# Tree-masked attention on one Trainium2 core: two halves of a PSUM bank for the transposed queries, and VectorE's V copies dealt evenly over the pairs

## The chip, the cores and the metric

The kernel runs on one core of a Trainium2 chip. The metric is the device time in microseconds (us) of one execution. A core has five engines that run their own instruction queues and wait for each other by semaphores: TensorE (PE in the profile; PEld is its weight load), VectorE (DVE), ScalarE (ACT), GpSimd (POOL) and SyncE (SP). Matmul results go to PSUM, everything else to SBUF; DMA engines move data between the chip's main memory and SBUF. Here nearly all DMAs are issued by POOL.

## The reference

Eight batches of twelve heads, 512 positions, 64 dimensions. Position i sees itself and its ancestors in a binary heap (parent of i is (i-1)//2), nothing else.

```python
scores = np.einsum('bhqd,bhkd->bhqk', Q, K) * scale      # scale = 1/8
scores = scores + (1 - mask) * (-1e9)                    # mask: self and ancestors
weights = np.exp(scores - np.max(scores, axis=-1, keepdims=True))
weights = weights / (np.sum(weights, axis=-1, keepdims=True) + 1e-10)
return np.einsum('bhqk,bhkd->bhqd', weights, V).astype(np.float32)
```

## The kernel before

The work is cut into 48 pairs of heads, six per batch. Since a query sees at most ten keys, the kernel doesn't compute all 512 x 512 scores. A first block of 128 keys (the upper levels of the tree) is scored against all 512 queries; the rest of the keys is met only by those queries that can have them as ancestors. Masks are added on TensorE by small code matrices (ctile) that put a large negative number where a query doesn't see a key.

Per pair i there are three functions:

- transposes(i): TensorE transposes Q (tile tq in PSUM, 8 matmuls, L293) and K (tile tk, 8 matmuls, L293). VectorE copies tq to the SBUF tile qt (L313), ScalarE copies tk to kt (L314). Both PSUM tiles have one buffer.
- scores(i): TensorE makes st (the first block, two matmuls with codes and two with qt and kt) and stx (the rest), all L339; ScalarE takes their exponentials to et (L352) and etx (L363). The PSUM tiles have one buffer each.
- values(i): TensorE multiplies et with v1 and etx with vx to o in PSUM (L391). A column of ones in v1 and vx gives the sums. VectorE takes the reciprocal (rec, L400) and the product (of, L405; called mult below).

V arrives in the staging tile vs as it lies in memory; its rows must be moved to other partitions. For a batch that is six copies by VectorE to vx ("big" in spread(), L279) and four by POOL to v1 ("small", also L279). Batches 0 and 1 do this in two halves of six heads (tile rows of 768 elements a partition), later batches all at once (1536). values() of a pair needs all six copies of its half or batch: batch 0's second half from pair 3 on, batch 1's halves from pairs 6 and 9, batch 2 from pair 12, batch 3 from pair 18.

The order of the instructions on TensorE, VectorE, ScalarE and POOL is that of the program text. The main loop over pairs is:

```python
            if i >= 4 and i + 2 < N:
                transposes(i + 2)
            if i + 1 < N:
                scores(i + 1)
            values(i)
            ...
            if i < 4:
                transposes(i + 2)
            for b, h0, h1, n0, n1 in deal.get(i, []):
                copies(spread(b, h0, h1)[0][n0:n1])
```

So from pair 4 on VectorE's order is qt(i+2), rec(i), mult(i), V copies of pair i. The dictionary deal says which of the six copies of which batch come in which pair: three in pairs 1 and 2 (batch 0's second half), 4 and 5, 7 and 8 (batch 1), 10 and 11 (batch 2); none in 0, 3, 6, 9 and 12; one in 13 to 16 and two in 17 (batch 3); then one in each pair to 41. The first six copies, batch 0's first half, come before the loop, after transposes(1).

POOL issues the loads (L233), up to twelve pairs ahead, and the stores (L412), which lag ten pairs behind while there are still loads; the last two pairs are stored by SP. The loads convert float32 to bf16 on the way.

Of the kernel before, what the change touches and what calls it, by code (L numbers as in the profile page):

```python
# [125 lines left out]
def kernel(  # L126
# [7 lines left out]
    nc = tc.nc  # L134
    B, H, S, D = Q.shape
    P = nc.NUM_PARTITIONS
    assert (S, D) == (512, 64) and H % 2 == 0
    T = 4
    HP = H // 2
# [4 lines left out]
    bf16 = mybir.dt.bfloat16  # L144
# [55 lines left out]
    psumT = ctx.enter_context(tc.tile_pool(name="psumT", bufs=1, space=PSUM))  # L200
    psumO = ctx.enter_context(tc.tile_pool(name="psumO", bufs=1, space=PSUM))


    plan = [(0, Q, 0, 0, 4), (0, K, 0, 0, 4), (0, V, 0, 0, 6),
            (0, Q, 0, 4, 8), (0, K, 0, 4, 8), (0, V, 0, 6, H),
# [3 lines left out]
    for b in range(2, B):  # L209
        at = HP * b - 2  # L210
        n = 4 if b < 3 else 6
# [5 lines left out]
        n = 8 if n == 4 else 6  # L217
        cuts = (n, H) if b < B - 1 else (n, 8, 10, H)
# [31 lines left out]
    def pick(v, t0, t1):  # L250

        stop = t1 + (1 if t1 > t0 else -1)
        return v[:, :, t0:stop if stop >= 0 else None:t1 - t0, :]

    def spread(b, h0, h1):
        vs = loaded["v", b]
        v1, vx = v1s[b % NV], vxs[b % NV]
        v = vs[:, h0:h1, :].rearrange("p h (t d) -> p h t d", t=T)
        big = [
            (vx[64:P, h0:h1, 0:3:2, 0:D], v[64:P, :, 0:3:2, :]),  # L260
            (vx[0:64, h0:h1, 1:4:2, 0:D], v[64:P, :, 1:4:2, :]),
        ]
        for part, c, t0, t1 in ((0, 0, 1, 2), (32, 0, 3, 0), (64, 1, 2, 1),
                                (96, 1, 0, 3)):
            assert KORD[XW[c] + part // 32] == (t0, 1)
            assert KORD[XW[c + 2] + part // 32] == (t1, 1)
            big.append((
                vx[part:part + 32, h0:h1, c:c + 3:2, 0:D],
                pick(v[32:64], t0, t1),
            ))  # L270
        small = [
            (v1[32 * r:32 * r + 32, h0:h1, 0:D], v[0:32, :, KORD[K1 + r][0], :])
            for r in range(T)
        ]
        return big, small

    def copies(ops, eng=None):
        for o, i in ops:
            (eng or nc.vector.tensor_copy)(out=o, in_=i)  # L279

    pairs = [(b, hp) for b in range(B) for hp in range(HP)]
    N = len(pairs)
    state, done, stored = {}, {}, []

    def transposes(i):
        b, hp = pairs[i]
        qs, ks = loaded["q", b], loaded["k", b]
        tq = psumT.tile([P, 512], bf16)
        tk = psumT.tile([P, 576], bf16)

        def put(o, src, t, mat):
            for hi in range(2):
                nc.tensor.matmul(  # L293
                    out=o[D * hi:D * hi + D], rhs=perms[mat],
                    lhsT=src[:, 2 * hp + hi, D * t:D * t + D],
                    start=True, stop=True, is_transpose=True,
                )

        for t in range(T):
            put(tq[:, P * t:P * t + P], qs, t, 0)  # L300
        for t in range(T):
            at = kput[t][1]
            if at[1] - at[0] == 32:
                step, run = at[2] - at[0], 64
            else:
                step, run = at[1] - at[0], 32
                assert at[2] - at[1] == step
            o = tk[:, at[0]:]
            o = bass.AP(o.tensor, o.offset, [list(o.ap[0]), [step, P // run], [1, run]])
            put(o, ks, t, 1 + t)  # L310
        qt = work.tile([P, 512], bf16)
        kt = work.tile([P, 512], bf16)
        nc.vector.tensor_copy(out=qt[:, :], in_=tq[:, :])  # L313
        nc.scalar.copy(  # L314
            out=kt[:, :].rearrange("d (i j x) -> d i j x", j=2, x=32),
            in_=tk[:, :].rearrange("d (j i x) -> d i j x", j=2, x=32)[:, 0:8],
        )
        state[i] = (qt, kt)

    def used(a):  # L320
        return a.rearrange("d (t p) -> d t p", t=T)[:, :, 32:P]

    def meeting(a, c):


        if c == 0:
            return a[:, 64:192]
        if c == 1:
            return a[:, 0:384].rearrange("d (n x) -> d n x", n=2)[:, :, 0:64]
        return a[:, P * c + 32:P * c + P]  # L330

    def scores(i):
        b, hp = pairs[i]
        q_, k_ = state[i]
        st1 = psumS.tile([P, 2, 512], fp32)
        stx = psumS.tile([P, 2, 512], fp32)

        def mm(dst, lhsT, rhs, first):
            nc.tensor.matmul(  # L339
                out=dst, lhsT=lhsT, rhs=rhs, start=first, stop=True,  # L340
                skip_group_check=not first,
            )

        hb = [slice(D * hi, D * hi + D) for hi in range(2)]
        q = [q_[hb[hi], :] for hi in range(2)]
        k = [k_[hb[hi], :] for hi in range(2)]
        for hi in range(2):
            mm(st1[:, hi, :], ck1[hb[hi], :], cq1[hb[hi], :], True)
        for hi in range(2):
            mm(st1[:, hi, :], k[hi][:, 32 * K1:32 * K1 + P], q[hi], False)  # L350
        et1 = et1pool.tile([P, 2, 512], bf16)
        nc.scalar.activation(  # L352
            out=et1[:, :, :], in_=st1[:, :, :], func=AF.Exp, scale=scale
        )
        for hi in range(2):
            mm(used(stx[:, hi, :]), ckx[hb[hi], :], cqx[hb[hi], :], True)
        for c in range(T):
            for hi in range(2):
                mm(meeting(stx[:, hi, :], c),
                   k[hi][:, 32 * XW[c]:32 * XW[c] + P],  # L360
                   meeting(q[hi], c), False)
        etx = etxs[i % NX]
        nc.scalar.activation(  # L363
            out=etx[:, :, :, 32:P],
            in_=stx[:, :, :].rearrange("p h (t q) -> p h t q", t=T)[:, :, :, 32:P],
            func=AF.Exp, scale=scale,
        )
        state[i] = (et1, etx)
# [40 lines left out]
    def store(eng, i, n):  # L409

        b, hp = pairs[i]
        eng.dma_start(  # L412
            out=out[b, 2 * hp:2 * hp + 2 * n].rearrange(
                "h (p t) d -> p h (t d)", t=T
            ),
            in_=done[i // 2][:, 2 * (i % 2):2 * (i % 2) + 2 * n, :],
        )
        stored.append(i)

    E = mybir.EngineType  # L420
    with tc.manual_schedule(engines={E.PE, E.DVE, E.Activation, E.Pool}):

        deal = {1: [(0, 6, H, 0, 3)], 2: [(0, 6, H, 3, 6)],
                4: [(1, 0, 6, 0, 3)], 5: [(1, 0, 6, 3, 6)],
                7: [(1, 6, H, 0, 3)], 8: [(1, 6, H, 3, 6)]}
        for b in range(2, B):
            cuts = ((4, 0, 3), (5, 3, 6)) if b == 2 else (
                (1, 0, 1), (2, 1, 2), (3, 2, 3), (4, 3, 4), (5, 4, 6))
            if b > 3:
                cuts = tuple((n, n, n + 1) for n in range(HP))  # L430
            for hp, n0, n1 in cuts:
                deal.setdefault(HP * (b - 1) + hp, []).append((b, 0, H, n0, n1))
        load(0, 14)
        transposes(0)
        scores(0)
        transposes(1)
        copies(spread(0, 0, 6)[0])
        for i in range(N):
            at_pair[0] = i
            load(i + AHEAD, FIRST[i] if i < len(FIRST) else None)  # L440
            upto = i - LATE if i + AHEAD < N - 1 else i - 1
            while 2 * len(stored) + 1 <= min(upto, N - 3):
                store(nc.gpsimd, 2 * len(stored), 2)
# [5 lines that stand above are left out]
            if i >= N - 2:  # L449
                store(nc.sync, i, 1)  # L450
            if i < 4:
                transposes(i + 2)
            for b, h0, h1, n0, n1 in deal.get(i, []):
                copies(spread(b, h0, h1)[0][n0:n1])
        assert not plan and not jobs

# [30 lines left out]
```

## Time and profile before

| | |
|---|---|
| median of 8 runs | 139.97 us (139.51 to 144.16) |
| the profiled execution's own time | 138.85 us |
| its span, first to last instruction | 137.1 us |
| TensorE busy | 109.3 us (80%) |
| ScalarE busy | 107.8 us (79%) |
| VectorE busy | 100.1 us (73%), of which V copies 38.1 (60 of them) |
| POOL busy | 90.3 us (66%) |
| DMA moved | 32.11 MB, mean 234 GB/s |
| rec(0), rec(12), rec(18), last rec | 15.28, 52.52, 66.86, 133.11 us |

Time inside the span is counted from its first instruction. rec(i) is the start of pair i's reciprocal, a convenient mark of progress: the first twelve pairs take 3.1 us each, the other 35 take 2.3. In a group's line of the profile stand the source line, the engine, the operation, output and inputs by tile name, the shape, the count, and then the busy time in us, the mean duration in ns and the engine's idle time before it.

### The profile page before, as it was taken

The page shows a single profiled execution, that of the slowest core. Times are in us where ns is not written, and L with a number is a line of the kernel's source. Part 1 is how long each engine was busy: PE and PEld are TensorE (multiplying, and loading weights), DVE is VectorE, ACT ScalarE, POOL GpSimd, SP SyncE. Part 2 cuts the span into 40 slices and gives each one's busy share as a digit, 9 for nine tenths or more (in the row PEclk, how much of TensorE's full clock was granted, in tenths as well). Part 3 has the DMA queues.
Part 4 walks back from the last instruction along what each step waited for, and adds up shares of the span by engine and source line. Part 5 has one row for each costly group of instructions (what it writes and reads, how often), then busy time and mean ns, then how long its engine had stood idle before and what let it go on. Part 6 is the DMA issues. An engine that isn't in the chain of part 4 may idle for free.

```text
span 137.1 us, 5468 instructions
## 1 busy us (share of the span) xinstructions
PE 109.3 (80%) x2400; PEld 79.6 (58%) x2400; DVE 100.1 (73%) x214; ACT 107.8 (79%) x145; POOL 90.3 (66%) x119
## 2 busy tenths in 40 slices
PE   0079687779957658998899998999889997999950
PEld 0035465556735536675677776776657675677630
DVE  4017668489797896979998897889877786975641
ACT  3027478697947965998899998999889997999940
POOL 6979895893697993339847397456944799921020
PEclk9999999999999999999999999999999999999995
DMA  4999999999999999999999999999999999999962
GB/s 79 162 188 196 196 197 196 198 197 198 197 199 196 204 193 198 198 253 225 197 318 241 274 202 206 338 228 259 197 265 294 248 294 274 386 391 387 360 243 99
DMA packets 41815, 32.11 MB, mean 234 GB/s; under 512 B 1280, under 2 KB 38784, under 8 KB 41792
## 3 DMA queue, kind: packets, MB, share of 16 engines
q0 software_dynamic: 41008, 30.94, 124.7%
q1 hardware_dynamic: 784, 0.84, 2.3%
q8 instruction: 18, 0.29, 0.8%
q14 instruction: 5, 0.04, 0.1%
HBM read 38.06 MB, written 12.58 MB: 369 GB/s over the span
## 4 chain that ended last, share of the span: by engine, by line
PE 49%; DVE 31%; ACT 6%; issue 6%; DMA 4%; POOL 1%; POOLq 0%
PE o L391 18%; DVE vx L279 16%; PE st L339 11%; DVE of L405 9%; PE stx L339 8%; PE tq L293 7%; PE tk L293 5%; DMA ks<-in_K_dram 4%; DVE qt L313 3%; ACT etx L363 3%; DVE rec L400 3%; ACT kt L314 2%; ACT et L352 1%; POOL qs L233 1%; POOLq L471 0%
## 5 line engine op out<-in xcount | busy, mean ns | idle before, releaser
L352 ACT ACTIVATE et<-st 128x1024 bf16<-128x1024 f32 x48 | 49.6, 1034 | 3.8 <-PE st L339 3.4
L314 ACT COPY kt<-tk 128x512 bf16<-128x512 bf16 x48 | 28.4, 592 | 19.3 <-PE tk L293 19.1
L279 DVE COPY vx<-vs 32x1536 bf16<-32x1536 bf16 (+3 forms) x60 | 38.1, 635 | 1.6
L363 ACT ACTIVATE etx<-stx 128x768 bf16<-128x768 f32 x48 | 39.2, 817 | 0.0
L405 DVE TENSOR_TENSOR of<-o,rec 128x512 f32<-128x512 f32 x48 | 33.2, 691 | 1.7
L279 POOL COPY v<-vs 32x768 bf16<-32x768 bf16 (+1 forms) x40 | 30.0, 750 | 2.7 <-DMA vs<-in_V_dram 0.9
L293 PE MATMUL tq<-ptile,qs 128*64 128x128 bf16 x384 | 19.9, 224 | 13.8 <-DVE qt L313 7.0
L391 PE MATMUL o<-vx,etx 128*64 128x65 bf16 (+1 forms) x576 | 26.8, 198 | 4.0 <-DVE vx L279 3.8
L412 POOL DMA_DIRECT2D out_dram<-of x23 | 18.2, 794 | 15.4 <-DVE of L405 8.2
L313 DVE COPY qt<-tq 128x512 bf16<-128x512 bf16 x48 | 20.0, 416 | 9.7 <-PE tq L293 9.0
L339 PEld LDWEIGHTS <-kt 64*128 64x128 bf16 x480 | 20.3, 96 | 10.6 <-ACT kt L314 3.5
L233 POOL DMA_DIRECT2D qs<-in_Q_dram x21 | 17.1, 813 | 13.3 <-PE o L391 4.0
L400 DVE RECIPROCAL rec<-o 128x8 f32<-128x8 f32 x48 | 9.8, 205 | 20.1 <-PE o L391 18.7
L293 PEld LDWEIGHTS <-qs 128*64 128x64 bf16 x384 | 15.2, 111 | 15.5 <-issue 8.0
L391 PEld LDWEIGHTS <-etx 128*64 128x64 bf16 (+1 forms) x576 | 19.5, 105 | 7.6 <-issue 5.0
L293 PE MATMUL tk<-ptile,ks 128*64 128x128 bf16 x384 | 20.3, 223 | 2.0 <-issue 1.3
L391 PE MATMUL o<-v,et 128*128 128x65 bf16 x384 | 20.4, 195 | 1.6 <-DVE of L405 1.1
L233 POOL DMA_DIRECT2D ks<-in_K_dram x21 | 16.6, 792 | 7.5 <-DMA vs<-in_V_dram 3.0
L339 PE MATMUL st<-qt,kt 64*128 64x512 bf16 x96 | 18.7, 386 | 2.0 <-DVE qt L313 1.8
L339 PE MATMUL st<-ctile 64*128 64x512 bf16 x96 | 19.2, 396 | 0.2 <-ACT et L352 0.2
L339 PEld LDWEIGHTS <-ctile 64*128 64x128 bf16 x192 | 11.3, 94 | 12.7 <-issue 1.8
L339 PE MATMUL stx<-qt,kt 64*128 64x96 bf16 (+1 forms) x384 | 17.8, 213 | 0.0
(13 smaller groups left out, 57.9 us busy)
## 6 DMA issues: line engine op xcount, KB each, us to landing
out_dram<-of POOLq DMA_DIRECT2D x23, 512.0 KB, 10.2
vs<-in_V_dram POOLq DMA_DIRECT2D x6, 768.0 KB, 15.8
qs<-in_Q_dram POOLq DMA_DIRECT2D x9, 384.0 KB, 15.7
ks<-in_K_dram POOLq DMA_DIRECT2D x9, 384.0 KB, 15.2
qs<-in_Q_dram POOLq DMA_DIRECT2D x9, 256.0 KB, 11.0
ks<-in_K_dram POOLq DMA_DIRECT2D x9, 256.0 KB, 11.5
vs<-in_V_dram POOLq DMA_DIRECT2D x4, 384.0 KB, 9.9
out_dram<-of SPq DMA_DIRECT2D x2, 256.0 KB, 2.1
```

The lines of the kernel that those rows point to most:

```text
L233: nc.gpsimd.dma_start(out=loaded[kind, b][:, h0:h1, :], in_=src[b, h0:h1].rearrange("h (p t) d -> p h (t d)", t=T),)
L279: (eng or nc.vector.tensor_copy)(out=o, in_=i)
L293: nc.tensor.matmul(out=o[D * hi:D * hi + D], rhs=perms[mat], lhsT=src[:, 2 * hp + hi, D * t:D * t + D], start=True, stop=True, is_transpos ...
L313: nc.vector.tensor_copy(out=qt[:, :], in_=tq[:, :])
L314: nc.scalar.copy(out=kt[:, :].rearrange("d (i j x) -> d i j x", j=2, x=32), in_=tk[:, :].rearrange("d (j i x) -> d i j x", j=2, x=32)[:, 0:8],
L339: nc.tensor.matmul(out=dst, lhsT=lhsT, rhs=rhs, start=first, stop=True, skip_group_check=not first,)
L352: nc.scalar.activation(out=et1[:, :, :], in_=st1[:, :, :], func=AF.Exp, scale=scale)
L363: nc.scalar.activation(out=etx[:, :, :, 32:P], in_=stx[:, :, :].rearrange("p h (t q) -> p h t q", t=T)[:, :, :, 32:P], func=AF.Exp, scale= ...
L391: nc.tensor.matmul(out=o2[p0:p1, hi, (D + 1) * t:(D + 1) * (t + 1)], lhsT=e[:, hi, P * t + p0:P * t + p1], rhs=v, start=hi not in (m[0] fo ...
L400: nc.vector.reciprocal(out=rec[:, :, :, :], in_=o4[:, :, :, D:D + 1])
L405: nc.vector.tensor_tensor(out=of4, in0=o4[:, :, :, 0:D], in1=rec[:, :, :, :].to_broadcast([P, 2, T, D]), op=ALU.mult,)
L412: eng.dma_start(out=out[b, 2 * hp:2 * hp + 2 * n].rearrange("h (p t) d -> p h (t d)", t=T), in_=done[i // 2][:, 2 * (i % 2):2 * (i % 2) + ...
```

## The change

Three edits, all in the order and the addresses of work; no instruction is added or removed.

1. The PSUM tile tq is no longer allocated per pair: one tile tqs of 2 x 512 bf16 elements is made once, and pair i uses its half i % 2. Both halves together are 2,048 bytes per partition.
2. The dictionary deal gives two V copies to each of pairs 0 to 11 and one to each of pairs 12 to 41.
3. Before the loop, four of the first six V copies come ahead of transposes(1), two after it.

```diff
+    tqs = psumT.tile([P, 2, 512], bf16)
...
     def transposes(i):
         b, hp = pairs[i]
         qs, ks = loaded["q", b], loaded["k", b]
-        tq = psumT.tile([P, 512], bf16)
+        tq = tqs[:, i % 2, :]
         tk = psumT.tile([P, 576], bf16)
...
-        nc.vector.tensor_copy(out=qt[:, :], in_=tq[:, :])
+        nc.vector.tensor_copy(out=qt[:, :], in_=tq)
...
-        deal = {1: [(0, 6, H, 0, 3)], 2: [(0, 6, H, 3, 6)],
-                4: [(1, 0, 6, 0, 3)], 5: [(1, 0, 6, 3, 6)],
-                7: [(1, 6, H, 0, 3)], 8: [(1, 6, H, 3, 6)]}
-        for b in range(2, B):
-            cuts = ((4, 0, 3), (5, 3, 6)) if b == 2 else (
-                (1, 0, 1), (2, 1, 2), (3, 2, 3), (4, 3, 4), (5, 4, 6))
-            if b > 3:
-                cuts = tuple((n, n, n + 1) for n in range(HP))
-            for hp, n0, n1 in cuts:
-                deal.setdefault(HP * (b - 1) + hp, []).append((b, 0, H, n0, n1))
+        deal = {}
+        for i in range(N):
+            b, hp = pairs[i]
+            if i < 9:
+                nb, h0, h1 = ((0, 6, H), (1, 0, 6), (1, 6, H))[i // 3]
+                deal[i] = (nb, h0, h1, 2 * (i % 3), 2 * (i % 3) + 2)
+            elif i < 12:
+                deal[i] = (2, 0, H, 2 * (i % 3), 2 * (i % 3) + 2)
+            elif b + 1 < B:
+                deal[i] = (b + 1, 0, H, hp, hp + 1)
         load(0, 14)
         transposes(0)
         scores(0)
+        big = spread(0, 0, 6)[0]
+        copies(big[:4])
         transposes(1)
-        copies(spread(0, 0, 6)[0])
+        copies(big[4:])
...
-            for b, h0, h1, n0, n1 in deal.get(i, []):
+            if i in deal:
+                b, h0, h1, n0, n1 = deal[i]
                 copies(spread(b, h0, h1)[0][n0:n1])
```

## The prediction

> **What bounds the kernel now.** I read the page first, then the chain of waits by stretch, then VectorE in order of time, then the DMA engines.
>
> The page's slices, DMA busy share in tenths and rate moved:
> ```profile
> DMA  4999999999999999999999999999999999999962
> GB/s 79 162 188 196 196 197 196 198 197 198 197 199 196 204 193 198 198 253 225 197 318 241 274 202 206 338 228 259 197 265 294 248 294 274 386 391 387 360 243 99
> ```
> The DMA engines never rest from about 5 to 130 us. While there are only loads (up to 57 us) they move a flat 197 GB/s; when only stores are left (116 to 127 us) some 386. Both are plateaus: the queue is full, and what is moved later can't be moved faster. So the kernel has two clocks, the compute pipeline and the DMA backlog, and a gain in the first counts only as far as the second lets it.
>
> The compute side in pairs 4 to 11, the chain of waits from 27.8 to 52.6 us, by line:
> ```profile
> by line: DVE vx L279 47.6%; DVE of L405 16.7%; PE o L391 12.2%; PE st L339 4.3%; DVE rec L400 4.2%; DVE qt L313 3.9%; PE tq L293 3.7%; issue 3.0%; PE stx L339 2.9%; PE tk L293 1.8%
> ```
> Nearly half of this stretch is V copies (L279) on VectorE. In order of time, pairs 7 to 9 of it (start, duration, instruction):
> ```profile
> 36.49 2.53 DVE L279 COPY vx<-vs 64x768 bf16<-64x768 bf16 x3
> 38.95 0.40 DVE L313 COPY qt<-tq 128x512 bf16<-128x512 bf16 x1
> 39.28 0.18 DVE L400 RECIPROCAL rec<-o 128x8 f32<-128x8 f32 x1
> 39.50 0.69 DVE L405 TENSOR_TENSOR of<-o,rec 128x512 f32<-128x512 f32 x1
> 40.22 1.85 DVE L279 COPY vx<-vs 32x768 bf16<-32x768 bf16 x3
> 42.10 0.42 DVE L313 COPY qt<-tq 128x512 bf16<-128x512 bf16 x1
> 42.66 0.21 DVE L400 RECIPROCAL rec<-o 128x8 f32<-128x8 f32 x1
> 42.91 0.69 DVE L405 TENSOR_TENSOR of<-o,rec 128x512 f32<-128x512 f32 x1
> 43.52 0.41 DVE L313 COPY qt<-tq 128x512 bf16<-128x512 bf16 x1
> 44.88 0.21 DVE L400 RECIPROCAL rec<-o 128x8 f32<-128x8 f32 x1 [0.94 <-PE o L391]
> ```
> From one reciprocal to the next: a pair with three V copies takes 3.4 us (39.28 to 42.66), its neighbour without any 2.2, and there VectorE idles 0.94. That is the unevenness that the new deal spreads. The same stretch's waits (us, times, longest):
> ```profile
> PE tq L293 <- DVE qt L313: 4.4, 3, 1.9
> DVE rec L400 <- PE o L391: 3.3, 3, 1.4
> PE o L391 <- DVE vx L279: 2.2, 2, 1.4
> ```
> The first is what the two halves are aimed at, the second is VectorE's idle time in the pairs without copies, the third is values() held by the last of three copies.
>
> Then the end, TensorE, load, VectorE, ScalarE, POOL, clock, DMA share and GB/s by stretch:
> ```profile
> 125.00:127.50 2.50, 2.50 (x66) 1.87 (x62) 1.60 (x5) 2.50 (x4) 0.76 (x1) 1.00 1.02 401
> 127.50:130.00 2.50, 2.25 (x40) 1.42 (x38) 1.66 (x4) 2.45 (x5) 0.00 (x0) 1.00 0.93 362
> 130.00:132.50 2.50, 1.38 (x37) 1.11 (x37) 0.94 (x3) 1.64 (x2) 0.75 (x1) 1.00 0.52 211
> 132.50:135.00 2.50, 0.57 (x19) 0.40 (x15) 0.90 (x2) 0.00 (x0) 0.00 (x0) 0.65 0.46 171
> 135.00:137.10 2.10, 0.00 (x0) 0.00 (x0) 0.00 (x0) 0.00 (x0) 0.00 (x0) 0.50 0.35 122
> ```
> Only here does the backlog run out and the DMA wait for compute. From 127.5 on 0.91 + 0.53 + 0.43 + 0.26 = 2.1 MB are moved; at the plateau of 386 GB/s that is 5.5 us, so the bytes alone would be done by 133.0, against about 135.8 now. **At most 2.8 us can be won at the end**, however early compute is.
>
> **The change part by part.** Times are of the profiled execution, which took 138.85 us with a span of 137.1; the median of the runs shown is 139.97, 1.1 above it. I carry the difference over to the median.
>
> *The halves (tqs).* The same 384 transposes and 48 copies of L313 (416 ns) remain; only the address alternates. Row first: TensorE waits 7.0 us in all for L313 before transposes, 8 times. If the wait went, pair i+3's transposes could start beside qt(i+2)'s copy; of the 7.0 us perhaps 0.5 is on the path, since behind the transposes the scores still need the same qt. The Trainium skill, "PSUM — Partial Sum Buffer", section "PSUM bank collisions raise a hardware error", speaks against it: TensorE writing and VectorE reading one bank in the same partitions collide also at different addresses, so PSUM must be guarded by bank, not by address. Both halves are one bank (2 x 1,024 bytes; the page gives 2 KiB per bank). No run here shows such an overlap. By the rule a safely guarded program keeps the wait and the halves bring 0; by the row 0.5. I take 0.
>
> *The prologue.* Now qt(1) ends at 11.65 and six copies follow, 11.69 to 14.69; values(0) waits for the last (TensorE goes on at 14.74). The first V half lands at 9.9 us (issued 2.89, 7.0 to landing), where VectorE is idle. After: four copies from 9.97, beside POOL's own V copies until 12.09. The nearest row is 64x768 beside POOL copies, 0.92 and 0.88 at 36.49, against 0.61 and 0.70 now; I take 0.8 twice, then 0.45 twice: until about 12.6. qt(1) queues behind them and ends at 13.0 in place of 11.65; scores(1), which began at 12.30 on ScalarE's kt, begins at 13.05; values(0), behind it on TensorE, begins at 14.3 in place of 13.54, and its second part, no longer held by copies, at 14.65 against 14.74. So 0. If every copy costs its undisturbed 0.36, qt(1) is hardly late: -0.55. If all are at 0.9: +0.6. A second rule speaks against this part. Row: matmul st takes 605 ns at 12.30 and 387 at 15.62; the durations step down near 13.8 (the clock column reads 1.00 on both sides, so the durations decide). "TensorE: Matmul & The Clock Gate", section "Part 1: The HAM clock gate", says that the clock doubles after a busy window of about 3.4 us. The new hole in TensorE's work, from about 12.2 to 13.05, lies in just that window, and one without a switch would cost another 3.4 us at the slow clock. In the slow stretch st to o takes 1.24 us (12.30 to 13.54), in the fast 0.68: by the rule up to 0.75 for about 1.3 pairs, by the trace 0 as long as the switch comes. I take 0 and keep 0.75 for the range.
>
> *Pairs 0 to 2.* Two copies each instead of 0, 3, 3. Pair 0 idled 1.57 us on VectorE before its next reciprocal: two copies (0.36 to 0.77) hide there. Pair 2 loses its third copy, which held values(3): the pair goes from 3.30 to the chain's 2.83 (mult, qt, st, stx, o, as in pairs 0 and 1): -0.45.
>
> *Pairs 3 to 11.* 18 copies, two a pair instead of 3, 3, 0. They took 2.64 + 4.31 + 4.82 = 11.8 us, 0.65 each. Pair 3's two hide in the 1.42 us idle before rec(4). From rec(4), 27.86, to rec(12), 52.52, is 24.66 us. After, VectorE has 8 x 1.36 (mult, qt, rec with gaps) and 16 copies at 0.65: 10.9 + 10.5 = 21.4. values(6), (9), (12) still wait for the last copy of their V, with VectorE idle about 0.2 each: 22.0. **-2.7.** No DMA or POOL instruction is moved.
>
> *Pairs 12 and 17.* Pair 12's new copy hides in 0.95 us idle; pair 17 loses one that took 0.55 or 1.08: -0.8. Later pairs are the same.
>
> Sum for compute: 0 - 0.45 - 2.7 - 0.8 = -3.95 by pair 18.
>
> *What then binds.* The loads keep their order behind a full queue, so they don't land earlier. The thinnest later lead is K of batch 6's second half: issued 88.51, landed 15.7 later at 104.2, used at 108.60: 4.4 us. 4.0 just fits. At the end the last mult would be done at about 130 instead of 134, with 1.1 MB still queued until 133.0: the 2.8 binds, less a few tenths because the last store is not spread evenly over the engines. Sum: **-2.45**, span 134.6, and 137.5 for the median.
>
> **The rivals.**
> A. *Compute gains less than the backlog would let through*: the prologue goes wrong with the slow clock (+1.35) and copies get dearer, a gain of 1 to 2: 138.0 to 139.0. For it: qt(1) does go behind four copies. Against: 3.95 leaves a reserve of 1.5.
> B. *Slower: each V copy collides with POOL.* A copy alone is 0.35 (768) or 0.55 (1536), beside POOL up to 0.92 and 1.08. POOL is busy 19.9 of 24.7 us in this stretch; copies in every pair could meet it each time. 16 copies at full price are 10 x 0.92 + 6 x 1.08 = 15.7, 5.2 over the sum: the 3.95 are gone and 1.2 is lost, 141.2. It decides from a mean of 0.9 per copy; now it is 0.65, and POOL's idle 32.2 to 35.5 us, where pairs 6 and 7 get copies, speaks against it.
> C. *No change*: the backlog ends later than I read it, or the early gain is lost to load leads: 140. Against: the DMA share falls to 0.5 after 130.
> D. *The halves do lift the wait*: 0.5 more for compute, swallowed by the same end: 137.3.
>
> **How the numbers follow.** A measurement of this kernel tells about 0.2% (0.28 us) from no change. Main case with D 0.62 (136.7 to 138.0), A 0.18, C 0.06, B 0.14. Faster 0.62 + 0.18 = 0.80, same 0.06, slower 0.14. The range starts at 136.6, the end's full 2.8 and some scatter of the median, and goes up through A to 139.5, leaving out C and B.
>
> **What would show it.** Right: about 2.2 to 2.9 us from each reciprocal to the next through pairs 4 to 11, none near 3.6; rec(12) at 48 to 50 us; waits of rec for o in 27.8 to 52.6 mostly gone; tq still waiting for qt; the DMA share near 1.0 until 132 or so, and the last store's wait for mult short against the backlog. qt(1) at 12 to 13 us. Wrong: V copies of 0.9 in every pair (B); transposes that wait for K before pair 40; a last mult at 130 with the DMA still idle afterwards, or a clock switch at 17 us.

## The result and the profile after

| | before | after |
|---|---|---|
| median | 139.51 us (53 runs, 137.78 to 144.80) | 137.73 us (18 runs, 137.30 to 138.08) |
| ratio after / before | | 0.9925, 95% interval 0.9905 to 0.9946 |
| profiled execution's own time | 138.85 us | 137.55 us |
| its span | 137.1 us | 135.8 us |
| rec(4), rec(12), rec(18), last rec | 27.86, 52.52, 66.86, 133.11 | 27.63, 48.49, 61.97, 130.16 |
| V copies on VectorE (60) | 38.1 us, mean 635 ns | 34.7 us, mean 578 ns |

The change is faster: by 0.75% in the ratio, by 1.3 us in the profiled executions, by 1.8 us in the medians. The ratio leaves out executions that lie more than 1.5% above their kernel's fastest, which before has and after has not; that is why the medians stand further apart than the ratio. (Source lines from the tq edit on are shifted by two: L279 is L281, L313 is L315, and so on.)

The even deal, in the chain of waits of the changed kernel from 27.6 to 48.5 us, its pairs 4 to 11:
```profile
by line: DVE vx L281 38.0%; DVE of L407 19.8%; PE o L393 11.9%; DVE qt L315 7.7%; PE st L341 5.2%; DVE rec L402 5.0%; PE tqs L295 4.2%; PE stx L341 3.4%; issue 3.3%; PE tk L295 2.1%
```
V copies are 38% of the chain instead of 48%, and of a stretch of 20.9 us instead of 24.7. VectorE in order of time, pairs 7 to 9:
```profile
35.46 1.74 DVE L281 COPY vx<-vs 32x768 bf16<-32x768 bf16 x2
37.22 0.42 DVE L315 COPY qt<-tqs 128x512 bf16<-128x512 bf16 x1
37.56 0.20 DVE L402 RECIPROCAL rec<-o 128x8 f32<-128x8 f32 x1
37.80 0.69 DVE L407 TENSOR_TENSOR of<-o,rec 128x512 f32<-128x512 f32 x1
38.52 1.25 DVE L281 COPY vx<-vs 32x768 bf16<-32x768 bf16 x2
39.80 0.43 DVE L315 COPY qt<-tqs 128x512 bf16<-128x512 bf16 x1
40.37 0.21 DVE L402 RECIPROCAL rec<-o 128x8 f32<-128x8 f32 x1
```
From rec to rec it is 2.8 us here (3.1 for the pair before), and none of these reciprocals waits. The waits of the stretch (us, times, longest):
```profile
PE tqs L295 <- DVE qt L315: 2.3, 4, 1.0
DVE rec L402 <- PE o L393: 1.3, 2, 1.1
PE o L393 <- DVE vx L281: 0.6, 2, 0.4
```
VectorE's wait for o fell from 3.3 to 1.3 us and TensorE's wait for the last V copy from 2.2 to 0.6. The transposes still wait for the copy of the other half.

The end, by stretch (TensorE, load, VectorE, ScalarE, POOL, clock, DMA share, GB/s; a DMA share of 1 is on average one packet in flight for each of the 16 engines, and it exceeds 1 where packets overlap):
```profile
127.50:130.00 2.50, 1.38 (x40) 1.19 (x40) 0.90 (x2) 1.19 (x2) 0.68 (x1) 1.00 1.01 397
130.00:132.50 2.50, 0.12 (x8) 0.00 (x1) 0.90 (x2) 0.00 (x0) 0.00 (x0) 1.00 0.97 373
132.50:135.00 2.50, 0.00 (x0) 0.00 (x0) 0.00 (x0) 0.00 (x0) 0.00 (x0) 0.60 0.34 119
```
From 130 to 132.5 the DMA share is 0.97 (0.52 before): the backlog, not the last mult, now sets the end. The last 0.3 MB still take until 134.9. Compute is 4.9 us ahead at rec(18), 3.0 at the last rec, and 1.3 is left at the end. The experiments ask where the rest went.

### The profile page after: what moved, and what is told of

The parts are those of the page before. It is cut to its first block, busy times and chain, and to the rows that moved or that the text cites. A ratio compares the mean times of both kernels' runs of the same rounds, so it can differ in the third digit from the quotient of the medians.

```text
span 135.8 us, 5468 instructions
## 1 busy us (share of the span) xinstructions
PE 110.7 (82%) x2400; PEld 80.5 (59%) x2400; DVE 97.1 (72%) x214; ACT 108.5 (80%) x145; POOL 90.6 (67%) x119
## 4 chain that ended last, share of the span: by engine, by line
PE 61%; DVE 21%; issue 5%; DMA 5%; ACT 2%; POOL 1%; POOLq 0%
PE o L393 22%; PE st L341 14%; PE stx L341 11%; DVE vx L281 9%; PE tqs L295 8%; DVE of L407 7%; PE tk L295 6%; DMA vs<-in_V_dram 5%; DVE qt L315 3%; DVE rec L402 2%; ACT kt L316 1%; POOL qs L235 1%; ACT etx L365 1%; POOL ks L235 1%; ACT et L354 0%
## 5 line engine op out<-in xcount | busy, mean ns | idle before, releaser
L316 ACT COPY kt<-tk 128x512 bf16<-128x512 bf16 x48 | 28.3, 589 | 14.2 <-PE tk L295 13.8
L281 DVE COPY vx<-vs 32x1536 bf16<-32x1536 bf16 (+3 forms) x60 | 34.7, 578 | 4.5 <-DMA vs<-in_V_dram 3.0
L281 POOL COPY v<-vs 32x768 bf16<-32x768 bf16 (+1 forms) x40 | 29.7, 742 | 2.9 <-DMA vs<-in_V_dram 1.2
L295 PE MATMUL tqs<-ptile,qs 128*64 128x128 bf16 x384 | 20.3, 226 | 10.5 <-DMA qs<-in_Q_dram 6.2
L315 DVE COPY qt<-tqs 128x512 bf16<-128x512 bf16 x48 | 20.0, 417 | 5.4 <-PE tqs L295 4.5
L295 PEld LDWEIGHTS <-qs 128*64 128x64 bf16 x384 | 15.3, 113 | 12.2 <-DMA qs<-in_Q_dram 6.2
L341 PE MATMUL st<-qt,kt 64*128 64x512 bf16 x96 | 18.8, 387 | 2.6 <-DVE qt L315 2.3
L341 PE MATMUL stx<-qt,kt 64*128 64x128 bf16 (+1 forms) x384 | 18.3, 213 | 0.2 <-issue 0.2
## 6 DMA issues: line engine op xcount, KB each, us to landing
qs<-in_Q_dram POOLq DMA_DIRECT2D x9, 384.0 KB, 15.8
ks<-in_K_dram POOLq DMA_DIRECT2D x9, 384.0 KB, 15.8
```

The lines of the kernel that those rows point to most:

```text
L295: nc.tensor.matmul(out=o[D * hi:D * hi + D], rhs=perms[mat], lhsT=src[:, 2 * hp + hi, D * t:D * t + D], start=True, stop=True, is_transpos ...
L315: nc.vector.tensor_copy(out=qt[:, :], in_=tq)
L316: nc.scalar.copy(out=kt[:, :].rearrange("d (i j x) -> d i j x", j=2, x=32), in_=tk[:, :].rearrange("d (j i x) -> d i j x", j=2, x=32)[:, 0:8],
L341: nc.tensor.matmul(out=dst, lhsT=lhsT, rhs=rhs, start=first, stop=True, skip_group_check=not first,)
```

## The experiments

Each ratio is to the kernel before in the same series; two series apart drift a little, so kernels of one series are compared.

**The three edits, one at a time.**

```diff
+    tqs = psumT.tile([P, 2, 512], bf16)
...
-        tq = psumT.tile([P, 512], bf16)
+        tq = tqs[:, i % 2, :]
...  # and the copy to qt reads this half
```


> The kernel before with the two halves alone. Theory 'one bank, one guard': TensorE still waits for VectorE's copy of the other half, so the waits of the transposes for L313's copy stay near 7 us in about 8 places, and the time is that of before within 0.2% (ratio 0.998 to 1.002). Rival 'the halves lift the wait': these waits go to nearly 0 and the ratio is 0.995 to 0.998.

Measured: 0.9972 (0.9944 to 0.9999), median 139.11. The waits of this kernel:
```profile
PE tqs L294 <- DVE qt L314: 6.9, 9, 1.9
```
7.0 us in 8 places before, 6.9 in 9 now. The halves lift nothing. (This execution had one clock drop, told of in the last section; it comes at 49 us.) The ratio's interval just misses 1; since no wait moved, I don't count the 0.3% as an effect of the halves, but the run doesn't exclude it.

```diff
-        deal = {1: [(0, 6, H, 0, 3)], ...
+        deal = {}                      # two a pair in 0 to 11, one in 12 to 41
```


> The kernel before with the even deal alone. Theory 'the deal is all of the gain': rec(12) starts near 48.5 us and rec(18) near 62 us (before 52.5 and 66.9), and the ratio to before is that of the whole change, 0.990 to 0.995. Rival 'the split prologue carries part of it': rec(12) near 48.5 too, but the ratio is nearer to 1 by 0.002 or more.

Measured: 0.9928 (0.9898 to 0.9959), median 137.97. rec(12) starts at 48.7, rec(18) at 61.8. The deal alone is the whole change, as far as intervals of 0.3% can tell.

```diff
+        big = spread(0, 0, 6)[0]
+        copies(big[:4])
         transposes(1)
-        copies(spread(0, 0, 6)[0])
+        copies(big[4:])
```


> The kernel before with the split prologue alone, four V copies ahead of pair 1's query copy. Theory 'late qt and late clock cancel what the copies win': rec(0) within 0.3 us of before (15.3), rec(1) the same or up to 0.5 later, ratio 0.999 to 1.003. Rival 'the prologue pays': rec(0) 0.5 or more earlier and ratio 0.997 or less.

Measured: 0.9963 (0.9928 to 0.9997), median 139.35; rec(0) at 15.4 and rec(1) at 18.4, no earlier than before (15.3 and 18.1). The trace speaks for the first theory. The ratio is below what it expected, but its interval nearly reaches 1 and nothing in the trace came earlier, so here too a small gain is neither shown nor excluded.

**Two instead of four copies ahead of qt(1).**
```diff
-        copies(big[:4])
+        copies(big[:2])
         transposes(1)
-        copies(big[4:])
+        copies(big[2:])
```


> The changed kernel with two instead of four V copies ahead of pair 1's query copy. qt(1) should end by about 11.8 us instead of 12.75, TensorE's hole before scores(1) (1.1 us) shrink to about 0.2, and st run fast from about 13.8 instead of 16.8. Theory 'the DMA backlog sets the end': rec(12) is up to 0.5 us earlier, the time stays that of the changed kernel (ratio to before 0.990 to 0.995). Rival 'compute sets the end': the time falls with rec(12), ratio 0.987 to 0.990.

Measured: 0.9929 (0.9902 to 0.9956), median 138.06, that is, as the deal alone in the same series. In the trace qt(1) ends at 11.4, and rec(0) starts at 14.3, a full microsecond before both kernels (against the kernel before, 0.6 of it is a start that was earlier anyway: its first st begins at 7.96 instead of 8.57); rec(12) is 0.7 earlier than in the changed kernel. Nothing of it reaches the end, where the last store lands at 135.2; this is the first theory. On the way K of batch 6's second half is now late:
```profile
104.48 0.41 PE L295 MATMUL tk<-ptile,ks 128*64 128x128 bf16 x8 [0.54 <-DMA ks<-in_K_dram]
```
Compute has run into the loads.

**Taking the backlog away.** In both kernels the six stores of pairs 24 to 35 are left out, so those outputs are not written.
```diff
     def store(eng, i, n):
+        if 24 <= i < 36:
+            stored.append(i)
+            return
```
The kernel before:

> The kernel before without the stores of pairs 24 to 35 (six of the 24 double-pair stores, 3.1 MB, about 8 us at the store rate); these outputs are not written. They are issued after pair 35, so that compute up to there is untouched and the DMA backlog at the end is gone. Both theories: the end follows compute, last reciprocal near 133 us as before, the span about 1 us shorter than before at most (135.5 to 137).

The changed kernel:

> The changed kernel without the same stores (outputs of pairs 24 to 35 not written). Theory 'the gain of compute is swallowed by the backlog at the end': without the backlog the end follows the last reciprocal, and this kernel is 2.5 to 4 us faster than the kernel before without these stores, against 1.0 to 1.8 with all stores. Rival 'compute itself gives the gain back after pair 18': the difference stays 1.0 to 1.8 us. If TensorE's stalls without a releaser are instruction fetches that queue behind the stores, they shrink from about 4 us to under 2.

Measured: before without these stores 1.0007 (0.9968 to 1.0046), median 139.58; after without them 0.9741 (0.9675 to 0.9806), median 135.59 (six runs only, 134.33 to 136.74). 3.1 MB less to move bring the old kernel nothing and the changed one 2.1 us. Between the two the gap is 2.7%, 3.7 us, against 0.75% with all stores. So compute's gain exists, and with all stores the backlog swallows more than half of it: the first theory. Clock drops (last section) don't hide a gain of the old kernel: among executions with a mean granted clock of at least 0.977 its medians are 139.01 without these stores and 138.91 with them. The rival holds in part: without these stores too, compute after rec(18) takes 67.8 us to the last rec instead of 66.3. (The old kernel's profiled execution had two drops of TensorE's clock, so its trace isn't set beside the other; its span was 139.7, beyond the expected 137. The changed kernel's profiled execution is the fastest of its six, and its rec(0) came at 13.65 us instead of 15.29, so its trace shows how it ends and not how large the gain is.) The end of the changed kernel without the backlog:
```profile
125.00:127.50 2.50, 1.57 (x34) 0.97 (x30) 1.34 (x3) 2.08 (x3) 0.75 (x1) 1.00 0.13 54
127.50:130.00 2.50, 0.77 (x20) 0.64 (x20) 1.03 (x3) 0.00 (x0) 0.00 (x0) 1.00 0.69 264
130.00:132.60 2.60, 0.00 (x0) 0.00 (x0) 0.00 (x0) 0.00 (x0) 0.00 (x0) 0.77 0.29 101
```
The DMA waits for compute (share 0.13), and the last store lands 2.1 us after its issue; with the backlog it takes 3.8. One expectation failed: TensorE's stalls without a releaser (places where the profile shows nothing that it waited for, marked "issue") stayed at 4.0 us.

**Parts of the deal.**
```diff
-            cuts = ((4, 0, 3), (5, 3, 6)) if b == 2 else (
+            cuts = ((3, 0, 2), (4, 2, 4), (5, 4, 6)) if b == 2 else (
```


> The kernel before with the even deal in pairs 9 to 11 alone (batch 2); pairs 1 to 8 and 12 to 17 keep 3, 3, 0 and 1, 1, 1, 1, 2. Theory 'TensorE's holes trip the clock': the kernels with the old deal show half the clock for 3.4 to 6.8 us after stretches in which TensorE is busy 1.7 to 1.8 of 3.5 us (36 to 39.5 and 46.5 to 50). Without the second hole the late drop at 50 us is gone, one at 40 can remain, and the slow times over 140.8 us get rarer than before. Plain sum by VectorE: rec(12) about 1 us earlier, and since without the drops compute sets the end of the old kernel, the ratio is 0.994 to 0.998.

Measured: 0.9966 (0.9933 to 0.9998), median 138.34, rec(12) at 51.3 (1.2 earlier), as the plain sum says. The profile shows no clock drop at 40 or at 50 us, and 2 of 22 times lie over 140.8 us, against 11 of 43 for the kernel before in this series.

```diff
-        deal = {1: [(0, 6, H, 0, 3)], 2: [(0, 6, H, 3, 6)], ...
+        deal = {}
+        for i in range(9):
+            nb, h0, h1 = ((0, 6, H), (1, 0, 6), (1, 6, H))[i // 3]
+            deal[i] = [(nb, h0, h1, 2 * (i % 3), 2 * (i % 3) + 2)]
```


> The kernel before with the even deal in pairs 0 to 8 alone (batches 0 and 1); pairs 10 and 11 keep three copies each. Theory 'TensorE's holes trip the clock': the hole of 46.5 to 50 us stays, so drops after it and some times over 140.8 us stay; the drop at 40 goes. Plain sum by VectorE: rec(9) about 2.2 us earlier than before, and of that at least 1.3 reaches the end, ratio 0.989 to 0.994 where there is no drop. Rival 'the whole even deal is needed': ratio 0.997 or more.

Measured: 0.9969 (0.9936 to 1.0003), median 138.32. rec(9) is 3.4 us earlier than before, more than expected, and yet the ratio is short of the 0.989 to 0.994 that I expected of it: the profile shows half the clock from 49.6 to 53.0 us, with the hole at 46.5 to 50 still there, and the last rec starts at 131.7. One of 22 times lies over 140.8 us. Each part alone brings about 0.3% (for this one the interval includes 1); together they bring 0.7%.

**Fewer bytes.**
```diff
-    nc.sync.dma_start(out=ptile[:, :], in_=perm_dram.ap())
+    nc.sync.dma_start(out=ptile[:, 0:P], in_=perm_dram.ap())
...  # the other four permutations and the second copy of the codes: VectorE copies
```


> The changed kernel with 200 KB less to load: of the permutation matrices only the identity is loaded and the other four are copied from it by VectorE, and the codes are loaded once and copied to the other partitions. Theory 'the DMA backlog sets the end': 0.2 MB at 390 GB/s are 0.5 us, the ratio falls by 0.003 to 0.005 against the changed kernel's 0.9925. Rival 'compute sets the end': no change, or as much as Q lands earlier (up to 0.3 us); TensorE's first transposes would show that.

Measured: 0.9897 (0.9842 to 0.9952) with six runs, median 137.83. Inconclusive: the last K lands 0.4 us earlier than in the changed kernel (at 117.1), as the bytes say, but this execution's compute was later (rec(1) at 18.8, the clock switching only at 18.6), and the last store lands at 135.3.

**A candidate, and the tail.** The last kernel's bytes, two copies ahead of qt(1), and LATE = 12, so that stores lag twelve pairs:

> A candidate from the runs so far: the changed kernel with two (not four) V copies ahead of pair 1's query copy, 200 KB less of constants to load, and stores lagging twelve pairs instead of ten so that K lands earlier against its use. If compute and backlog both end early, the last mult is done by about 130 us and the last store lands near 134.4: ratio to before 0.986 to 0.991, median about 137.3. If the backlog drains as unevenly as now, ratio 0.990 to 0.994, no better than the changed kernel.

Measured: 0.9897 (0.9865 to 0.9928), median 137.75. The last mult is done at 130.3, but the last store lands at 135.2, so the backlog drains as before. In this series the kernel before had a median of 140.76, so the ratio flatters; by its median and its fastest run (137.18) it is the changed kernel again. No version beat it.

```diff
-            if i >= N - 2:
-                store(nc.sync, i, 1)
+            if i == N - 1:
+                store(nc.gpsimd, N - 2, 2)
```


> The changed kernel with the last two pairs stored by one DMA of POOL (512 KB, packets of 4 KB) after the last mult, instead of two of SyncE with packets of 1 KB. Theory 'the sixteen engines drain the backlog unevenly': the last landing stays at 134.5 to 136 us, ratio 0.992 to 0.997. Rival 'small packets of a second queue make the tail': the landing comes by 134, ratio 0.986 to 0.990.

Measured: 0.9973 (0.9937 to 1.0009), median 138.63, slower than the changed kernel by its median. The store was issued only at 132.6, so that a landing by 134 was out of reach, and the answer comes from the store before it, with nothing from SyncE beside it:
```profile
127.50:130.00 2.50, 1.38 (x37) 1.11 (x37) 1.00 (x3) 1.66 (x2) 0.75 (x1) 1.00 0.98 383
130.00:132.50 2.50, 0.77 (x19) 0.51 (x15) 0.90 (x2) 0.00 (x0) 0.00 (x0) 1.00 0.62 247
132.50:135.00 2.50, 0.00 (x0) 0.00 (x0) 0.00 (x0) 0.00 (x0) 0.75 (x1) 0.53 0.51 208
```
The store issued at 127.9 lands at 134.0. In half microseconds:
```profile
131.00:131.50 0.50, 0.29 (x6) 0.17 (x5) 0.17 (x1) 0.00 (x0) 0.00 (x0) 1.00 0.72 287
131.50:132.00 0.50, 0.00 (x0) 0.00 (x0) 0.47 (x2) 0.00 (x0) 0.00 (x0) 1.00 0.25 98
132.00:132.50 0.50, 0.00 (x0) 0.00 (x0) 0.26 (x1) 0.00 (x0) 0.00 (x0) 1.00 0.15 57
132.50:133.00 0.50, 0.00 (x0) 0.00 (x0) 0.00 (x0) 0.00 (x0) 0.44 (x1) 0.66 0.12 49
133.00:133.50 0.50, 0.00 (x0) 0.00 (x0) 0.00 (x0) 0.00 (x0) 0.31 (x1) 0.50 0.10 41
```
From 131.5 on the DMA share is 0.25 and less; 0.12 is the work of two of 16 engines. Most engines are done, and the landing waits for the last. With SyncE's two stores beside it, in the changed kernel, the same store landed at 133.6. So the tail is an uneven drain of the queue and no matter of small packets. Which engines are late, the trace doesn't tell.

## Why the prediction was right, and what was off

The time lay in the range (137.73 in 136.6 to 139.5) and on the forecast side; the main case, an early pipeline held by the DMA backlog, is what the runs without stores show. By its steps:

- *Halves 0*: held; alone, they left the wait at 6.9 us of 7.0. That agrees with what the Trainium skill, "PSUM — Partial Sum Buffer", section "PSUM bank collisions raise a hardware error", says of guarding by bank. The run shows that the wait stays, not that the bank is the reason: both halves are also one tile of the program.
- *Prologue 0*: held, its working too: qt(1) ended at 12.76 (13.0 forecast), st began at 12.81 (13.05), the second part of values(0) at 14.48 (14.65). TensorE's new hole and the late clock:
```profile
12.81 0.61 PE L341 MATMUL st<-qt,kt 64*128 64x512 bf16 x2 [1.11 <-DVE qt L315]
16.04 0.61 PE L341 MATMUL st<-ctile 64*128 64x512 bf16 x2
16.79 0.45 PE L341 MATMUL st<-qt,kt 64*128 64x512 bf16 x2
17.08 0.32 PE L341 MATMUL stx<-ctile 64*128 64x384 bf16 x2
```
  The matmuls speed up at 16.8 instead of 13.8, and rec(1) comes 3.07 after rec(0) instead of 2.83. So the late clock, whose cost I had set to 0, took at least 0.24 here, within the 0.75 kept for it. It isn't a certain cost. The same scores matmuls in the changed kernel without stores, where the hole was 0.37 us, and with two copies ahead of qt(1), where there was none:
```profile
12.13 0.39 PE L341 MATMUL st<-qt,kt 64*128 64x512 bf16 x2 [0.37 <-DVE qt L315]
11.69 0.39 PE L341 MATMUL st<-qt,kt 64*128 64x512 bf16 x2
```
  Both ran fast. The hole at this place sorts the 13 profiles: where it is 0.6 to 1.2 us (four kernels, all with four copies ahead) the clock rises between 16.1 and 18.6 us, where it is smaller or absent between 11.6 and 14.5. So of the signs of being wrong one came, a clock switch at 17 us, and it cost little.
- *Pair 2*: -0.45 forecast; the pair took 2.83 as said.
- *Pairs 3 to 11*: right in kind, too small. rec(4) to rec(12) took 20.86 against the 22.0 forecast. The term that was off is the V copy: 16 of them took 9.4 us, 0.59 each and not 0.65. Rival B, dearer copies, did not come about (its full price was read too low: the longest copy before, at 62.09 us beside POOL, takes 1.21 and not 1.08).
- *Pairs 12 and 17*: -0.8 forecast, -0.9 measured (13.48 from 14.34).
- *Load lead*: 4.4 less 4.0 was to just fit. K, issued at 88.55, landed 15.8 later at about 104.4, and was used at 104.59.
- *What was missing*: after pair 18 compute gave 1.9 of its 4.9 us back; I had put this at nothing ("Later pairs are the same"). From rec(18) to the last rec TensorE was busy 62.3 us and idle 5.9, before 61.8 and 4.5. Of the idle time, its matmuls stood for 4.1 us at places with no releaser (tk 1.6, stx 1.1, o 0.9, tqs 0.5, from 62 to 131 us) against 1.8 before; the last section says what these stalls go with. Two of them:
```profile
73.75 0.22 PE L393 MATMUL o<-vx,etx 128*64 128x65 bf16 x1 [0.63 <-issue]
122.84 0.33 PE L341 MATMUL stx<-ctile 64*128 64x384 bf16 x1 [0.95 <-issue]
```
- *The end, the step that failed in size*: I gave the drain a few tenths over the plateau rate. From 127.5 on 2.2 MB were left, 5.8 us at 386 GB/s, so until 133.3. The end of the changed kernel in half microseconds:
```profile
132.50:133.00 0.50, 0.00 (x0) 0.00 (x0) 0.00 (x0) 0.00 (x0) 0.00 (x0) 1.00 0.94 336
133.00:133.50 0.50, 0.00 (x0) 0.00 (x0) 0.00 (x0) 0.00 (x0) 0.00 (x0) 0.51 0.42 148
133.50:134.00 0.50, 0.00 (x0) 0.00 (x0) 0.00 (x0) 0.00 (x0) 0.00 (x0) 0.50 0.19 68
134.00:134.50 0.50, 0.00 (x0) 0.00 (x0) 0.00 (x0) 0.00 (x0) 0.00 (x0) 0.50 0.12 43
```
  The last packets move at 134.5, with two or three of the 16 engines at work. The uneven drain thus costs 1.2 us, not the few tenths (0.35) that I had allowed. (The store counts as landed 0.4 later, at 134.9; before, the last packets moved at 135.8 and landed at 136.2.) Another 0.3 us is 0.1 MB more in the queue than the forecast had. So the end came 1.3 us earlier, not 2.45.
- *The median*: 137.5 forecast, 137.73 measured, and closer than the sum deserves. I carried a distance of 1.1 us from the profiled execution to the median over; after the change it is 0.2. The profiled executions differ by 1.3, not by 2.45; what the prediction took too much there, the medians made good, probably because clock drops (last section) no longer lengthen them. That the forecast of the median came so close is luck.

## What to carry to other kernels

Spread side work over all iterations of an in-order engine before looking for anything cleverer: the same 60 copies, dealt evenly, brought pairs 4 to 11 from 24.7 to 20.9 us. Then ask of any gain what stands behind it: here a DMA queue that is full from 5 to 130 us turned 3.7 us of compute into about 1, and leaving a few transfers out of both versions is a cheap way to see that. At the end of a full queue, count on the slowest DMA engine, not on bytes by rate.

## What was not expected of the hardware

The clock drop. Three kernels with the old deal were profiled (the halves alone, the prologue alone, before without stores) with TensorE's clock at half for 3.4 or 6.8 us after pairs 7 to 8 or 10 to 11, and so was the kernel that keeps the old deal in pairs 10 and 11. The halves alone:
```profile
46.50:50.00 3.50, 1.62 (x28) 1.10 (x29) 3.39 (x7) 1.63 (x4) 3.42 (x5) 0.91 1.45 199
50.00:53.50 3.50, 2.71 (x46) 2.02 (x43) 3.09 (x6) 1.64 (x3) 2.12 (x3) 0.50 1.45 199
```
and the changed kernel:
```profile
46.50:50.00 3.50, 3.15 (x68) 2.22 (x65) 3.25 (x6) 3.07 (x5) 3.42 (x5) 1.00 1.46 199
```
TensorE (the first number) is busy 1.62 of 3.5 us, and half the clock (0.50 in the clock column) follows; in that kernel rec(12) to rec(13) took 3.6 us instead of 2.2. Busy 3.15, no drop. The Trainium skill, "TensorE: Matmul & The Clock Gate", section "Part 1: The HAM clock gate", tells of a free-running window of about 3.4 us; that fits a drop that comes in some executions and not in others, for the profile of before has the same hole without it. None of the profiles with the whole even deal shows a drop, and their times stay within about 1.5 us (137.37 to 138.88 for the deal alone, 14 runs; only the six without stores spread over 2.4), while the halves alone spread from 137.86 to 142.79. The clock goes with the time: of 169 further executions of the kernel before, the 78 with a mean granted clock under 0.972 have medians of 140.9 to 141.9 us by series, the 75 at 0.977 or more 138.9 to 139.5. That the holes trip the clock is an inference from these profiles; evening only pairs 9 to 11 left times up to 143.6, with a hole at 37 us still there. Nor is it shown that the even deal ends all drops: 4 of the 14 executions of the deal alone have mean clocks of 0.964 to 0.968, lower than its profiled 0.985, and yet times of 137.88 to 138.88. A drop there may cost little because the backlog sets the end.

The stalls. TensorE's stalls without a releaser last 0.2 to 1 us each. DMA queue 8, which the profile labels "instruction", moves 18 packets of 16 KB, mostly some 6 us apart. One begins at 95.58 us (first line, DMA packets from 95.5 to 96.6), and TensorE's next stall ends at 97.83:
```profile
q8 instruction: 1, 0.02, 5.5%
97.83 0.36 PE L295 MATMUL tk<-ptile,ks 128*64 128x128 bf16 x6 [0.71 <-issue]
```
The 13 profiles have 79 such stalls of over 0.15 us from 13 us on, and every one ends 2.2 to 2.6 us after such a packet began. That ties the stalls to the fetching of instructions; that TensorE waits for the fetched instructions themselves is an inference from these times. Why some come late, and why more of them do after the change (7 stalls against 4), is open. Leaving stores out didn't shorten the stalls, and fewer TensorE instructions weren't tried.
